# Alternating two token halves, and two PSUM banks, matmul by matmul, in a decoder trunk

## The chip, the cores and the metric

The kernel runs on one core of one Trainium2 chip. The metric is the device time of one execution in microseconds, as the median of several runs. A profile of one execution shows what each engine did: TensorE (PE for matmuls, PEld for the loading of stationary operands), VectorE (DVE), ScalarE (ACT), GpSimd (POOL) and the DMA queue of SyncE (SP).

## What is computed

A two-layer decoder trunk over 256 tokens with a model width of 2048, all in float32. Layer 0 projects into an RG-LRU group and an HGRN2 group, concatenates their outputs and projects back; layer 1 is attention with three dilated windows. Each is followed by a squared-ReLU MLP of width 8192. The large products are these:

```python
def trunk(x):                                   # x: 256 x 2048
    h = x + recurrent_mixers(rms(x), w_in, ..., w_out)    # w_in 2048 x 6144, w_out 2048 x 2048
    h = h + square(relu(rms(h) @ w1[0])) @ w2[0]          # w1 2048 x 8192, w2 8192 x 2048
    h = h + dilated_attention(rms(h), w_qkv, w_o)         # w_qkv 2048 x 6144, w_o 2048 x 2048
    h = h + square(relu(rms(h) @ w1[1])) @ w2[1]
    return rms(h)
```

## The kernel before

**Three products for one.** Weights and activations are float32, and each is held as a sum of two numbers of the faster matmul type: `hi`, the rounded value, and `lo`, the rest. A product is then three matmuls: high by high, high by low, low by high. The activations lie feature-major in `bufa` and `bufb` (128 partitions, 16 blocks of 128 features, the 256 tokens' high parts and then their low parts).

**Weights.** They come in units of 1 MB (128 x 2048) into `raw`, three buffers, on SyncE's queue. `Weights.split` (L97, L98) makes the two parts, in halves of 1024 columns: ScalarE casts `raw` to `hi`, VectorE subtracts to get `lo`. `hi` and `lo` have five half-unit buffers each, so a cast waits until TensorE has finished with the half that lay in its buffer, two and a half units back.

**Two kinds of product.** `project` keeps a weight block stationary and moves the 256 tokens; it fills one PSUM tile with 128 output features for all tokens, in some 5.5 us. `tokens` keeps activations stationary (128 features of 128 tokens) and moves 512 weight columns, and so fills two PSUM tiles, `ps[0]` for the first 128 tokens and `ps[1]` for the last 128, each one bank of 128 x 512 float32. Both take their tiles from the pool `pmm`, which has three, in turn; the five other banks belong to other pools. `tokens` is called for the HGRN and the attention values (`tokens_group`; evacuated by ScalarE at L314), for both output projections (`out_project`: w_out and w_o, four calls each), and for the MLP's second product (w2, four calls after each 16 calls of `project`, four times in a layer). A call goes through four units `g`, each with four blocks `i` of features: 4 x 4 x 2 halves x 3 products = 96 matmuls, 24 for each unit.

**Order.** All matmuls made by `mm` (L146) and the transposes made by `turn` (L149) are chained in program order on TensorE. The other engines' orders are laid out by the compiler by priority: evacuations are urgent, the weight stream comes next.

**After a call.** `add_res` (L553) adds `ps[0]` and then `ps[1]` to the residual `xres` on VectorE, one instruction for each half, which frees the two PSUM tiles. After `out_project`'s calls, and the last four of an MLP, the new columns are squared for the norm (L258) and transposed back to feature-major into `bufa` (`to_features`, L149, L203 and L204); that work is put off (`later`) and carried out by `flush` after the next call's first unit, or after 12 of the next `project`'s 16 blocks. The last four calls of the second MLP are multiplied by the final gain instead (L607), and each half's final norm (L719 to L725) and scaling (L729, L731) follow before the output DMAs (L733).

Of the kernel before, what the change touches and what calls it, by code (L numbers as in the profile page):

```python
# [19 lines left out]
P = 128  # L20
S = 256
# [19 lines left out]
def trunk_kernel(ctx, tc, x, xtok, cols, tab, masks, pos, fin, w_in, w_gate, w_out, w_qkv, w_o, w1, w2, out):  # L41
# [19 lines left out]
    bufa = act.tile([P, KB, 2 * S], F32R, name="bufa")  # L61
# [10 lines left out]
    for step in ORDER.split():  # L72
        src, first, n = where[step[0]]
# [9 lines left out]
    at = [0, 0]  # L83
# [51 lines left out]
    def unit(src, i):  # L135
        u = at[1]
        assert units[u][0] is src and units[u][1] == i, (u, i)
        at[1] += 1
        if u + 2 >= at[0]:
            fetch()  # L140
        return made.pop(u)
# [3 lines left out]
    def mm(*args, **kw):  # L145
        chain[:] = [after(T.matmul(*args, **kw), chain)]  # L146
# [6 lines left out]
    def flush():  # L153
        todo = later[:]
        later.clear()
        for f in todo:
            f()

    def after(ins, names):
        ins = getattr(ins, "ins", ins)  # L160
        for n in names:
            tc.add_manual_dep(ins, n, NOSYNC, reason="order on one engine")
        return ins.name
# [113 lines left out]
    def rstd(nrm):  # L277
        r = tmp.tile([P, 2], F32, name="nr2", bufs=2)
        rsqrt(r, nrm.mean(), 2)
        return r  # L280
# [7 lines left out]
            V.scalar_tensor_tensor(t, t, -0.5, v, op0=OP.mult, op1=OP.mult)  # L288
            V.scalar_tensor_tensor(r, t, 1.5, r, op0=OP.add, op1=OP.mult)

    def tokens(src, i0, mov, kgs=(0, 1, 2, 3), by_k=False):
        ps = [pmm.tile([P, 512], F32, name="p") for _ in range(2)]
        for g in kgs:
            w = unit(src, i0 + g)
            order = [(j, i) for i in range(4) for j in range(2)] if by_k else \
                [(j, i) for j in range(2) for i in range(4)]
            for j, i in order:
                k = 4 * g + i
                h, l = w.part(i * 512, 512)
                xh = mov[:, k, j * P:j * P + P]  # L300
                xl = mov[:, k, S + j * P:S + j * P + P]
                first, last = g == kgs[0] and i == 0, g == kgs[-1] and i == 3
                mm(ps[j], xh, h, start=first, stop=False)
                mm(ps[j], xh, l, start=False, stop=False)
                mm(ps[j], xl, h, start=False, stop=last)
            flush()
        return ps

    def tokens_group(src, i0, rt=None, by_k=False):
        ps = tokens(src, i0, bufa, by_k=by_k)  # L310
        v = vgs.tile([P, 2, 512], F32, name="vg", bufs=2)
        with urgent():
            for j in range(2):
                A.activation(v[:, j], ps[j], AF.Copy, scale=1.0 if rt is None else rt[:, j:j + 1])  # L314
        return v
# [16 lines left out]
    rt = rstd(nrm)  # L332
# [64 lines left out]
        return t.rearrange("p (n two c) -> p n two c", two=2, c=c)[:, :, int(second), :]  # L397

    def hgrn_v(i):
        v = tokens_group(w_in, 16 + i * 16, rt if i else None, by_k=not i)  # L400
        if not i:
            for j in range(2):
                A.activation(v[:, j], v[:, j], AF.Copy, scale=rt[:, j:j + 1])
        return v
# [133 lines left out]
    for step in ORDER.split():  # L538
        i = int(step[1])
        if step[0] == "v":  # L540
            vgroups[i] = hgrn_v(i)
        elif step[0] == "h":
            hgrn(i, vgroups[i // 4])
        else:
            {"x": lru_in, "y": lru_out, "g": lru_gates}[step[0]](i)
# [26 lines left out]
    def out_project(src, gname, kgs):  # L572
        nrm = Norm()
        for n in range(4):
            add_res(tokens(src, 4 * n, bufb, kgs), n, nrm)
            to_features(n, gname)
        return nrm
# [6 lines left out]
    def mlp(layer, nrm, nxt, gname):  # L584
        r2 = None
        for q in range(4):
            for m in range(16):
                z = folded(project(w1, layer * 64 + q * 16 + m, bufa), "z")
                with urgent():
                    V.scalar_tensor_tensor(z, z, 0.0, z, op0=OP.max, op1=OP.mult)  # L590
                    split_to(bufb[:, m], z)
                if r2 is None:
                    r2 = nrm.inv_mean()
                    if not gname:
                        lut(spare, epsc, AF.Sqrt)
                    spot[:] = [after(V.memset(spare, 0.0), [])]
            for n in range(4):
                ps = tokens(w2, layer * 64 + q * 16 + 4 * n, bufb)
                add_res(ps, n, nxt if q == 3 else None, r2)
                if q == 3:  # L600
                    if gname:
                        to_features(n, gname)
                    else:
                        at = slice(n * 512, n * 512 + 512)
                        with urgent():
                            for j in range(2):
                                V.tensor_tensor(xres[:, j, at], xres[:, j, at], fing[:, at], OP.mult)  # L607
# [36 lines left out]
    rt = rstd(nx1)  # L644
# [46 lines left out]
    for g in range(4):  # L691
        if g < 3:
            vg = tokens_group(w_qkv, g * 12, rt)
        for hd in range(4 * g, 4 * g + 4):
            u0 = g * 12 + (4 if g < 3 else 0) + (hd % 4) * 2
            st = scores(u0)
            if g < 3:
                mix(hd, st, vg)
            else:
                pend.append(st)  # L700
    vg = tokens_group(w_qkv, 44, rt)
    for hd, bank in zip(range(12, 16), (("po", 1), ("pd", 1), ("pl", 2), ("pl", 2))):
        mix(hd, pend[hd - 12], vg, *bank)
# [10 lines left out]
    for j in range(2):  # L714
        m = tmp.tile([P, 1], F32, name="fm", bufs=2)
        r = tmp.tile([P, 1], F32, name="fr", bufs=2)
        t = tmp.tile([P, 1], F32, name="ft", bufs=2)
        with urgent():
# [7 lines left out]
            for h in range(4):  # L726
                at = slice(h * 512, h * 512 + 512)
# [113 lines left out]
```

## Time and profile before

| | |
|---|---|
| median of 3 runs | 2237.13 us (2237.09 to 2237.16) |
| the profiled execution | 2237.57 us, span 2235.8 us, granted clock 0.999 |
| PE busy | 2218.4 us, 99% of the span, 12196 matmuls |
| PEld busy | 1935.1 us, 87%, 12196 loads |
| DVE busy | 1410.6 us, 63% |
| ACT busy | 1074.4 us, 48% |
| matmuls `p<-hi,bufb` and `p<-lo,bufb` of 128 x 512 (w2, w_out, w_o) | 2560 of 390 ns and 1280 of 389 ns |
| casts to `hi` (L97), splits to `lo` (L98) of 128 x 1024 | 770 of 1051 ns, 770 of 1223 ns |
| `add_res` (L553), with and without a scale | 64 of 748 ns, 16 of 688 ns |

A matmul's row is its whole passage, and the next one begins before it ends, so rows of 390 ns follow each other closer than that; starts are compared, not durations. In a tile's name the operand named first after the arrow is the moving one: `p<-hi,bufb` moves high weights over stationary activations. A number in brackets at the end of a row of the timeline is the idle time of the engine before it, with what ended it.

### The profile page before, as it was taken

The numbers are of one execution on the slowest core, as the hardware profiler recorded it, in microseconds if no ns is written. First come the engines' busy times: TensorE is split into PE (matmuls) and PEld (weight loads), VectorE is DVE, ScalarE is ACT, GpSimd is POOL, SyncE is SP. The second block draws the span as 40 slices with busy tenths as digits, with TensorE's granted clock in tenths as the row PEclk, the third lists the DMA queues.
The fourth block names the chain that finished last, engine by engine and source line by source line (L and its number), as shares of the span: only waits on it lengthen the run. The fifth ranks groups of instructions, "written<-read, shape, count | busy, mean of one in ns | idle before, by whom it ended". The sixth has DMA issues, their size and how long they took to land.

```text
span 2235.8 us, 30376 instructions
## 1 busy us (share of the span) xinstructions
PE 2218.4 (99%) x12196; PEld 1935.1 (87%) x12196; DVE 1410.6 (63%) x2220; ACT 1074.4 (48%) x1540; POOL 1.9 (0%) x7
## 2 busy tenths in 40 slices
PE   9999999999999999999999999999999999999998
PEld 8999998888888888888888888888888888888886
DVE  7777886665565565465567878556655645655654
ACT  6444585554444344354554445455434434444543
POOL 0000000000000000000000000000000000000000
PEclk9999999999999999999999999999999999999999
DMA  8444445455555555555554444555555555555553
GB/s 309 151 154 168 152 154 205 172 191 191 200 188 188 190 190 189 199 193 188 188 188 167 172 170 170 191 186 188 189 188 191 191 193 196 189 188 190 190 192 125
DMA packets 58717, 414.51 MB, mean 185 GB/s; under 512 B 6528, under 2 KB 7296, under 8 KB 9168
## 3 DMA queue, kind: packets, MB, share of 16 engines
q1 hardware_dynamic: 58320, 412.20, 51.9%
q8 instruction: 95, 1.56, 0.3%
q0 software_dynamic: 256, 0.38, 0.1%
q14 instruction: 46, 0.38, 0.1%
HBM read 410.70 MB, written 2.10 MB: 185 GB/s over the span
## 4 chain that ended last, share of the span: by engine, by line
PE 98%; ACT 1%; DVE 1%; DMA 0%; issue 0%; SPq 0%; ACTq 0%; DVEq 0%
PE p L146 94%; PE pl L440 1%; PE pl L149 0%; PE pl L665 0%; DMA raw<-in_w_in 0%; PE po L686 0%; PE pd L678 0%; ACT hi L97 0%; DVE bufa L204 0%; ACT L169 0%; DVE lo L98 0%; PE pd L424 0%; PE pl L664 0%; ACT gi L169 0%; PE po L687 0%
## 5 line engine op out<-in xcount | busy, mean ns | idle before, releaser
L98 DVE TENSOR_TENSOR lo<-raw,hi 128x1024 fp32r<-128x1024 f32 (+1 forms) x774 | 932.5, 1220 | 602.7 <-ACT hi L97 435.2
L97 ACT CAST hi<-raw 128x1024 fp32r<-128x1024 f32 (+1 forms) x774 | 811.3, 1049 | 876.7 <-PE p L146 798.7
L146 PE MATMUL p<-bufa,hi 128*128 128x512 f32 (+1 forms) x3840 | 858.2, 357 | 2.4 <-DVE bufa L204 2.4
L146 PE MATMUL p<-hi,bufb 128*128 128x512 f32 x2560 | 792.5, 390 | 0.0
L146 PEld LDWEIGHTS p<-bufa,hi 128*128 128x128 f32 x3840 | 671.9, 189 | 94.8 <-DVE bufa L204 3.5
L146 PEld LDWEIGHTS p<-hi,bufb 128*128 128x128 f32 x2560 | 480.7, 188 | 99.1
L146 PE MATMUL p<-bufa,lo 128*128 128x256 f32 x3200 | 520.0, 284 | 0.0
L146 PE MATMUL p<-lo,bufb 128*128 128x512 f32 x1280 | 498.1, 389 | 0.0
L146 PEld LDWEIGHTS p<-bufa,lo 128*128 128x128 f32 x3200 | 451.9, 191 | 12.3
L146 PEld LDWEIGHTS p<-lo,bufb 128*128 128x128 f32 x1280 | 240.4, 188 | 49.2
L201 DVE TENSOR_TENSOR bufb<-z,bufb 128x256 fp32r<-128x256 f32 x136 | 57.7, 424 | 126.5 <-ACT bufb L200 126.5
L146 PE MATMUL p<-hi,bufa 128*128 128x512 f32 x384 | 122.5, 395 | 0.5 <-ACT hi L97 0.5
L193 ACT COPY t<-p 128x256 f32<-128x256 f32 x128 | 47.6, 372 | 110.0 <-PE p L146 110.0
L146 PEld LDWEIGHTS p<-hi,bufa 128*128 128x128 f32 x384 | 72.2, 188 | 16.1 <-ACT hi L97 1.5
L146 PE MATMUL p<-lo,bufa 128*128 128x512 f32 x192 | 76.4, 398 | 1.6 <-DVE lo L98 1.6
L200 ACT CAST bufb<-z 128x256 fp32r<-128x256 f32 x136 | 54.5, 401 | 17.2 <-DVE z L590 14.4
L553 DVE SCALAR_TENSOR_TENSOR xall<-p,nm,xall 128x512 f32<-128x512 f32 x64 | 47.9, 748 | 19.8 <-PE p L146 19.8
L590 DVE SCALAR_TENSOR_TENSOR z<-z 128x256 f32<-128x256 f32 x128 | 54.5, 426 | 4.4
L195 DVE TENSOR_TENSOR z<-p,t 128x256 f32<-128x256 f32 x128 | 53.5, 418 | 0.0
L258 ACT ACTIVATE z<-xall 128x512 bf16<-128x512 f32 x32 | 20.2, 631 | 53.3 <-DVE xall L553 52.6
L146 PEld LDWEIGHTS p<-lo,bufa 128*128 128x128 f32 x192 | 36.1, 188 | 10.3 <-DVE lo L98 3.6
L440 PE MATMUL pl<-qk 128*128 128x64 f32 x224 | 30.9, 260 | 0.0
(199 smaller groups left out, 730.1 us busy)
## 6 DMA issues: line engine op xcount, KB each, us to landing
raw<-in_w SPq DMA_DIRECT2D x256, 1024.0 KB, 4.8
raw<-in_w_qkv SPq DMA_DIRECT2D x48, 1024.0 KB, 4.8
raw<-in_w_in SPq DMA_DIRECT2D x46, 1024.0 KB, 4.8
raw<-in_w_out SPq DMA_DIRECT2D x16, 1024.0 KB, 4.8
raw<-in_w_o SPq DMA_DIRECT2D x16, 1024.0 KB, 4.8
xall<-in_xtok SPq DMA_DIRECT2D x1, 2048.0 KB, 9.3
raw<-in_w_gate SPq DMA_DIRECT2D x2, 1024.0 KB, 4.8
out<-xall SPq DMA_DIRECT2D x4, 512.0 KB, 3.3
```

Source lines behind the costliest of these rows:

```text
L97: A.copy(h, w)
L98: V.tensor_tensor(l, w, h.bitcast(F32), OP.subtract)
L146: chain[:] = [after(T.matmul(*args, **kw), chain)]
L193: A.copy(t, p[:, S:])
L195: V.tensor_tensor(z, p[:, :S], t, OP.add)
L200: A.copy(dst[:, :S], src)
L201: V.tensor_tensor(dst[:, S:], src, dst[:, :S].bitcast(F32), OP.subtract)
L258: A.activation(q, xres[:, j, n * 512:n * 512 + 512], AF.Square, accum_out=self.ss[:, j, n:n + 1])
L440: T.matmul(pl[:, j], kq[:, js], halves(qp[:, js], c, True), start=True, stop=True)
L553: V.scalar_tensor_tensor(xres[:, j, at], ps[j], 1.0 if scale is None else scale[:, j:j + 1], xres[:, j, at], op0=OP.mult, op1=OP.add)
L590: V.scalar_tensor_tensor(z, z, 0.0, z, op0=OP.max, op1=OP.mult)
```

## The change

In `tokens` the loop over the two halves becomes the innermost. Before, each unit went through all four blocks for the first half (12 matmuls into `ps[0]`) and then for the second (12 into `ps[1]`); the first HGRN value group alone (`by_k`) changed halves after each block's three products. After, for each block and each of the three products, one matmul goes into `ps[0]` and the next into `ps[1]`. The number of matmuls, their operands and their shapes are the same. Within a unit, the first half of the weights (blocks 0 and 1) is used by the first 12 matmuls instead of by matmuls 1 to 6 and 13 to 18. The argument `by_k` goes.

```diff
-    def tokens(src, i0, mov, kgs=(0, 1, 2, 3), by_k=False):
+    def tokens(src, i0, mov, kgs=(0, 1, 2, 3)):
         ps = [pmm.tile([P, 512], F32, name="p") for _ in range(2)]
         for g in kgs:
             w = unit(src, i0 + g)
-            order = [(j, i) for i in range(4) for j in range(2)] if by_k else \
-                [(j, i) for j in range(2) for i in range(4)]
-            for j, i in order:
+            first, last = g == kgs[0], g == kgs[-1]
+            for i in range(4):
                 k = 4 * g + i
                 h, l = w.part(i * 512, 512)
-                xh = mov[:, k, j * P:j * P + P]
-                xl = mov[:, k, S + j * P:S + j * P + P]
-                first, last = g == kgs[0] and i == 0, g == kgs[-1] and i == 3
-                mm(ps[j], xh, h, start=first, stop=False)
-                mm(ps[j], xh, l, start=False, stop=False)
-                mm(ps[j], xl, h, start=False, stop=last)
+                for n, (at, m) in enumerate(((0, h), (0, l), (S, h))):
+                    for j in range(2):
+                        mm(ps[j], mov[:, k, at + j * P:at + j * P + P], m, start=first and not i and not n,
+                           stop=last and i == 3 and n == 2)
             flush()
         return ps
```

`tokens_group` and `hgrn_v` lose the argument `by_k` that they passed on.

More of the change, by code (lines that the diff above doesn't have):

```diff
@@ L294, in tokens, with tokens_group @@
             w = unit(src, i0 + g)
-            order = [(j, i) for i in range(4) for j in range(2)] if by_k else \
-                [(j, i) for j in range(2) for i in range(4)]
-            for j, i in order:
+            first, last = g == kgs[0], g == kgs[-1]
+            for i in range(4):
                 k = 4 * g + i
                 h, l = w.part(i * 512, 512)
-                xh = mov[:, k, j * P:j * P + P]
-                xl = mov[:, k, S + j * P:S + j * P + P]
-                first, last = g == kgs[0] and i == 0, g == kgs[-1] and i == 3
-                mm(ps[j], xh, h, start=first, stop=False)
-                mm(ps[j], xh, l, start=False, stop=False)
-                mm(ps[j], xl, h, start=False, stop=last)
+                for n, (at, m) in enumerate(((0, h), (0, l), (S, h))):
+                    for j in range(2):
+                        mm(ps[j], mov[:, k, at + j * P:at + j * P + P], m, start=first and not i and not n,
+                           stop=last and i == 3 and n == 2)
             flush()
         return ps
-    def tokens_group(src, i0, rt=None, by_k=False):
-        ps = tokens(src, i0, bufa, by_k=by_k)
+    def tokens_group(src, i0, rt=None):
+        ps = tokens(src, i0, bufa)
         v = vgs.tile([P, 2, 512], F32, name="vg", bufs=2)
@@ L399, in hgrn_v @@
     def hgrn_v(i):
-        v = tokens_group(w_in, 16 + i * 16, rt if i else None, by_k=not i)
+        v = tokens_group(w_in, 16 + i * 16, rt if i else None)
         if not i:
```

## The prediction

> **What bounds the kernel now.** I read the busy shares and the chain of the page first, then the timeline around one boundary between two token groups, then the places where TensorE really waits.
>
> ```profile
> PE 2218.4 (99%) x12196; PEld 1935.1 (87%) x12196; DVE 1410.6 (63%) x2220; ACT 1074.4 (48%) x1540; POOL 1.9 (0%) x7
> PEclk9999999999999999999999999999999999999999
> PE 98%; ACT 1%; DVE 1%; DMA 0%; issue 0%; SPq 0%; ACTq 0%; DVEq 0%
> ```
>
> TensorE is the path, at full clock (0.999 granted), so the end moves only if the spacing of its matmuls changes or if a new idle gap opens. PE and PEld have the same count: every matmul loads its own weights, also where two in a row have the same stationary block, so the change breaks up no shared load. The next fence is TensorE's timeline across the boundary of two groups of `tokens` (the last matmul of one starts at 538.67, the first of the next 0.23 later, inside the same row of two).
>
> ```profile
> 537.99 0.61 PE L146 MATMUL p<-hi,bufb 128*128 128x512 f32 x2
> 538.44 0.39 PE L146 MATMUL p<-lo,bufb 128*128 128x512 f32 x1
> 538.67 0.61 PE L146 MATMUL p<-hi,bufb 128*128 128x512 f32 x2
> 539.12 0.39 PE L146 MATMUL p<-lo,bufb 128*128 128x512 f32 x1
> 539.35 0.61 PE L146 MATMUL p<-hi,bufb 128*128 128x512 f32 x2
> 539.80 0.39 PE L146 MATMUL p<-lo,bufb 128*128 128x512 f32 x1
> ```
>
> Triples follow each other every 0.68 us, 226.7 ns a matmul, and the one that holds a change of bank is no different. VectorE over the same place:
>
> ```profile
> 536.38 0.75 DVE L553 SCALAR_TENSOR_TENSOR xall<-p,nm,xall 128x512 f32<-128x512 f32 x1 [0.41 <-PE p L146]
> 538.82 1.22 DVE L98 TENSOR_TENSOR lo<-raw,hi 128x1024 fp32r<-128x1024 f32 x1 [1.69 <-ACT hi L97]
> 539.96 0.74 DVE L553 SCALAR_TENSOR_TENSOR xall<-p,nm,xall 128x512 f32<-128x512 f32 x1
> 540.62 1.22 DVE L98 TENSOR_TENSOR lo<-raw,hi 128x1024 fp32r<-128x1024 f32 x1
> ```
>
> The first half's tile is evacuated (L553) 39 ns after its last matmul, which is the 12th before the end of the group; the second half's waits 0.9 us behind a weight split. Neither delays TensorE: `ps[1]` of the next group is not touched before that group's 13th matmul.
>
> **Steady rate: no change (0 us).** `tokens` is called 46 times with 96 matmuls, 4416 of the 12196. In the six undisturbed w2 stretches I took the start-to-start time at each of the 96 positions: where the bank changes (after every 12th) it is 226.6 ns, elsewhere 226.5 to 226.8 (the first five of a group up to 229). A wide matmul has a fixed part of 13 ns: 512 columns take 226.7, 256 take 120.0, so 256 columns are 106.7 and 226.7 - 2 x 106.7 = 13.3. If it came from writing the same bank twice running, it would be gone at each of those changes; it isn't.
>
> **New wait: the third buffer.** `pmm` has three tiles, handed out in turn (the compiled kernel before takes banks 0, 2, 1 throughout). A group holds A and B; the next gets C, then A. Before, A's last matmul and its next first one are 24 matmuls (5.4 us) apart. After, they are three apart: A last, B last, C first, A first. Between the two lies the evacuation of A. Call C's first start 0, by rows:
> - A's last matmul starts two steps earlier, at -0.453, and its row is 0.389 long: end -0.064.
> - L553 starts 0.039 later and takes 0.751 (w2) or 0.692 (w_out, w_o; no scale): end 0.726 or 0.667.
> - TensorE restarts 0.053 after it, as here, where a matmul waits for VectorE (L204 ends at 431.255, in the run of four from 430.77):
>
> ```profile
> 431.31 0.49 PE L146 MATMUL p<-bufa,hi 128*128 128x512 f32 x1 [0.65 <-DVE bufa L204]
> 430.77 1.95 DVE L204 SCALAR_TENSOR_TENSOR bufa<-pl,c__82,bufa 128x256 fp32r<-128x256 f32 x4
> 431.31 0.19 PEld L146 LDWEIGHTS p<-bufa,hi 128*128 128x128 f32 x1 [0.89 <-DVE bufa L204]
> ```
>
> The matmul and its weight load start together: the wait holds the load back too, so the load is exposed. The matmul is 0.49 long instead of 0.39, and after the second such wait (432.335) the next two start 0.337 and 0.236 later instead of 0.227: 0.12 us more. So A's first matmul starts at 0.779 instead of 0.227: 0.55 + 0.12 = 0.67 us a boundary in w2, 0.61 in w_out and w_o.
>
> Boundaries: 3 in each of 8 w2 passes, 24 x 0.67 = 16.1; 3 each in w_out and w_o, 6 x 0.61 = 3.7; the last value group of w_qkv is followed directly by w_o, there ScalarE evacuates (L314, 0.687): 0.6. Where a feature-major `project` stands on either side there is no cost: it uses one tile for about 5.5 us, and the tile that is needed has long been read.
>
> **Who else stands in VectorE's queue.** Each unit's 24 matmuls free the first half of its weights at the 18th matmul before, at the 12th after; ScalarE's cast (L97) and VectorE's split (L98) hang on that and move 6 x 0.227 = 1.36 us earlier. The split above ends at 540.04; moved, at 538.68. A's last matmul ends at 538.81, so L553 finds VectorE free, by 0.13 us. That margin is thin; without it the wait grows up to the 0.91 by which the second L553 is late now (its rival is below).
>
> **Ends of the kernel.** At the end, the first half's L553, final gain, norm and scaling run under the last 12 matmuls today. After, both halves come together: 0.75 + 0.69 (L607) + 2 x 0.48 (L731) + 7 x 0.16 = 3.5 us of VectorE work is moved behind the last matmul, of which part fills VectorE's idle time between 2225.3 and 2230.9, where it waits for ScalarE. Between 0 and 3.5 I take 1.5, nearer to the lower half because the second half's chain is mostly waits. At the start, the group already alternated by threes; one more matmul gets ahead of the wait for `lo` at 21.66: -0.2 (bounds -0.7, three such waits, and 0). The residual transposes (L149) come after the next group's first 24 matmuls, 5.4 us, and both L553 are done after 1.5: nothing.
>
> **Sum.** 16.1 + 3.7 + 0.6 + 1.5 - 0.2 = 21.7 us. The profiled execution took 2237.57 (span 2235.8): 2259.3; it lies 0.44 above the median, so the prediction is 2237.1 + 21.7 = 2258.8. Without the exposed load and the tail (31 x 0.12 + 1.5 less) it is 2253.6.
>
> A rule speaks against the change: the Trainium skill, "Perfetto Trace Analysis", section "Matmuls", asks that independent groups rotate through banks so that the evacuation of one overlaps the next one's matmuls. The trace before shows just that; with two groups open and three banks there is one bank left to rotate into.
>
> **Rivals.**
> - *Banks help, faster.* If writing alternate banks takes the fixed 13.3 ns off every matmul, 4416 x 13.3 = 58.7 less, 21.7 more: 2200. It wins once a step falls by 21.7 / 4416 = 4.9 ns, below 221.8. For it: the fixed part has no explanation in the rows. Against: 226.6 at every existing change of bank. Chance 0.08. The Trainium skill, "TensorE: Matmul & The Clock Gate", section "Back-to-back issue gap", gives N/2.4 + 2.5, 215.7 ns for 512 columns; the trace shows 11 more, and an estimate by that page would be 4416 x 11 = 48.6 us less if the change recovered it.
> - *The split stays in front of L553.* VectorE's order is fixed when the kernel is compiled; if the moved split starts 0.13 us or more too late, L553 begins up to 0.91 late at each of 31 boundaries: up to 28 more, 2268 to 2287. For it: this is what the second L553 shows before. Against: the earlier release. Chance 0.12.
> - *No wait.* Bank A is read in time after all, or the change alters no order that matters: 2236 to 2240. Against: 0.75 of evacuation can't fit in the 0.29 us between A's last end and its next start. Chance 0.04.
>
> **Numbers.** Forecast (the wait of 0.55 to 0.8 at about 31 boundaries, 2252 to 2268): 0.76. With the second rival slower is 0.88; 0.2% (4.5 us) is about what a measurement can tell from no change. The range 2252 to 2282 takes in the forecast and most of the second rival.
>
> **What would show it.** The waits view should have about 24 "PE p L146 <- DVE xall L553" of 0.5 to 0.6 us, 13 in sum, and six or seven smaller; TensorE's busy time nearly unchanged, triples still every 0.68 us. Rows of 512 columns closer than 222 ns would prove me wrong on the banks, waits of 1.5 us with L98 in front of L553 on the queue, no waits for L553 at all on the buffers.

## Result and profile after

The changed kernel takes 2262.23 us (2262.11 to 2262.34) against 2237.14 (2237.09 to 2237.16): 1.0112 times as long, 95% interval 1.0095 to 1.013, 25.1 us more. The profiled execution has a span of 2260.5 against 2235.8, 24.7 more (the execution profiled before lay 0.4 above its median); the lines of the changed kernel stand three earlier (`add_res` is L550). From the page after, the busy times, the clock and the chain:

```profile
PE 2228.0 (99%) x12196; PEld 1931.5 (85%) x12196; DVE 1409.8 (62%) x2220; ACT 1072.0 (47%) x1540; POOL 1.9 (0%) x7
PEclk9999999999999999999999999999999999999999
PE 95%; DVE 2%; ACT 2%; issue 0%; DMA 0%; SPq 0%; ACTq 0%; DVEq 0%
```

The same work at the same clock. TensorE's share of the chain fell from 98% to 95%; VectorE's and ScalarE's rose from 1% to 2% each, and `add_res` (L550), which the chain's list of lines did not have before, now stands in it with 1%: something waits for it. TensorE's timeline over the boundary that the prediction showed, now 2.66 us later:

```profile
540.65 0.62 PE L146 MATMUL p<-lo,bufb 128*128 128x512 f32 x2
541.11 0.84 PE L146 MATMUL p<-hi,bufb 128*128 128x512 f32 x3
542.34 0.50 PE L146 MATMUL p<-hi,bufb 128*128 128x512 f32 x1 [0.39 <-DVE xall L550]
542.68 0.64 PE L146 MATMUL p<-lo,bufb 128*128 128x512 f32 x2
```

The row of three holds the last two matmuls of one group and the first of the next. Then the second of the next group, which wants the tile A, starts at 542.34, 0.779 us after the first; before, the distance was 0.227. It is 0.50 long instead of 0.39, and the next starts 0.341 later instead of 0.227. VectorE and the weight loads there:

```profile
540.13 1.23 DVE L98 TENSOR_TENSOR lo<-raw,hi 128x1024 fp32r<-128x1024 f32 x1 [1.50 <-ACT hi L97]
541.53 1.41 DVE L550 SCALAR_TENSOR_TENSOR xall<-p,nm,xall 128x512 f32<-128x512 f32 x2 [0.18 <-PE p L146]
```

```profile
542.34 0.19 PEld L146 LDWEIGHTS p<-hi,bufb 128*128 128x128 f32 x1 [0.81 <-DVE xall L550]
```

VectorE has finished its split and stands idle for 0.18 us until A's last matmul ends; then both halves are added one behind the other. The load for A's first matmul waits with the matmul. The waits view collects it:

```profile
PEld p L146 <- DVE xall L550: 24.8, 31, 0.8
PE p L146 <- DVE xall L550: 11.8, 31, 0.4
PEld p L146 <- DVE z L377: 1.7, 1, 1.7
```

A column of 11.8 us for TensorE undersells it: idle time counts from the modelled end of the matmul before, which lies 0.39 after its start, while the pace is a start every 0.227. The starts of the same matmul in both traces say what each place costs:

| where | later by, us |
|---|---|
| start and first HGRN value group | -0.9 |
| first w_out group, a wait for the tile of the last y block but one | 1.65 |
| 24 boundaries of w2, 0.69 to 0.73 each | 16.9 |
| 3 + 3 boundaries of w_out and w_o, 0.63 to 0.67 each | 3.9 |
| w2's last group to the first value group of w_qkv | 0.7 |
| last value group of w_qkv to the first w_o group | 0.6 |
| after the last matmul | 1.8 |

They add to the 24.7. At the first w_out group TensorE waits for VectorE's evacuation of a y block (L377); at the first w_o group it waits for ScalarE's evacuation of the value group (L311):

```profile
336.57 0.50 PE L146 MATMUL p<-hi,bufb 128*128 128x512 f32 x1 [1.38 <-DVE z L377]
336.10 0.42 DVE L377 TENSOR_TENSOR z<-p,nr 128x256 f32<-128x256 f32 x1
1438.21 0.70 PE L683 MATMUL po<-pT,vg 128*128 128x256 f32 x2 [0.33 <-ACT vg L311]
```

The matmul that waits in the last row is not w_o's second one but a product of the attention heads that reads the evacuated values `vg`. Before, it stood behind w_o's first eleven matmuls; now it stands behind the first alone. All other stages have the same length in both to within 0.06 us, and between the 31st and the last matmul of an undisturbed group the mean distance of two starts is 226.67 ns in both traces.

### The profile page after: what moved, and what is told of

Read it like the earlier page. It is cut to its first block, busy times and chain, and to the rows that moved or that the text cites. A ratio compares the mean times of both kernels' runs of the same rounds, so it can differ in the third digit from the quotient of the medians.

```text
span 2260.5 us, 30371 instructions
## 1 busy us (share of the span) xinstructions
PE 2228.0 (99%) x12196; PEld 1931.5 (85%) x12196; DVE 1409.8 (62%) x2220; ACT 1072.0 (47%) x1540; POOL 1.9 (0%) x7
## 4 chain that ended last, share of the span: by engine, by line
PE 95%; DVE 2%; ACT 2%; issue 0%; DMA 0%; SPq 0%; ACTq 0%; DVEq 0%
PE p L146 92%; DVE xall L550 1%; PE pl L437 1%; ACT hi L97 0%; PE pl L149 0%; PE pl L662 0%; ACT L169 0%; PE po L683 0%; DVE lo L98 0%; ACT gi L169 0%; PE pd L675 0%; DMA xall<-in_x 0%; ACT bufa L203 0%; DVE bufa L204 0%; PE pd L421 0%
## 5 line engine op out<-in xcount | busy, mean ns | idle before, releaser
L146 PE MATMUL p<-hi,bufb 128*128 128x512 f32 x2560 | 697.7, 391 | 12.8 <-DVE xall L550 11.4
L146 PE MATMUL p<-lo,bufb 128*128 128x512 f32 x1280 | 394.9, 390 | 0.0
L146 PE MATMUL p<-hi,bufa 128*128 128x512 f32 x384 | 109.1, 396 | 1.2 <-ACT hi L97 0.8
L146 PE MATMUL p<-lo,bufa 128*128 128x512 f32 x192 | 60.1, 394 | 1.1 <-DVE lo L98 1.1
L550 DVE SCALAR_TENSOR_TENSOR xall<-p,nm,xall 128x512 f32<-128x512 f32 x64 | 45.1, 746 | 16.5 <-PE p L146 16.1
L437 PEld LDWEIGHTS pl<-qk 128*128 128x128 f32 x224 | 30.1, 191 | 0.3
```

The costliest lines, as they stand in the source:

```text
L437: T.matmul(pl[:, j], kq[:, js], halves(qp[:, js], c, True), start=True, stop=True)
L550: V.scalar_tensor_tensor(xres[:, j, at], ps[j], 1.0 if scale is None else scale[:, j:j + 1], xres[:, j, at], op0=OP.mult, op1=OP.add)
```

## Experiments

The theory: the loss is the evacuation of A, between two matmuls that the new order brings within three of each other, plus the waits and the tail that come from both halves ending together. The rival: alternating banks or stationary blocks at every matmul is slow by itself.

**Four tiles, and the control for it.** The edit in the changed kernel, and in the kernel before:

```diff
-    pmm = pool("pmm", 3, space=PSUM)
+    pmm = pool("pmm", 4, space=PSUM)
...
-        p = psc.tile([P, 512], F32, name="pt", bufs=1)
+        p = psc.tile([P, 512], F32, name="pd", bufs=1)
...
-        pt = psc.tile([P, 2, P], F32, name="pt", bufs=1)
+        pt = psc.tile([P, 2, P], F32, name="pd", bufs=1)
```

> The changed kernel with four tiles in the pool pmm instead of three (the bank comes from the tile pt, whose uses move to pd). Theory (A's evacuation sits between two matmuls that are only three apart): with four tiles the next group takes two others, no matmul waits for add_res, the 24.7 us between the two traces shrink to the tail (+1.8) and the start (-0.9): about 2238 us. Rival (writing two banks alternately, or changing the stationary block every time, is slow by itself): all matmuls still alternate, so it stays at about 2262.

> The kernel before with the same four tiles in pmm and pt merged into pd. Control for the other run: the kernel before waits nowhere for a tile of pmm, so both theories expect 2237 us, within 0.5, unless sharing pd costs something in the HGRN heads; what it costs there has to be taken off the other run too.

Measured: 2291.29 us (2290.71 to 2292.64) and 2290.79 (2290.21 to 2291.23). Both totals missed: merging `pt` into `pd` costs the kernel before 53.7 us. But the two differ by 0.5 us where the kernels they come from differ by 25, and between their traces no boundary from the second w_out group on is longer; only the tail is, by 1.82. So the loss goes when neighbouring groups share no tile, though the control's own cost makes this a weak proof, and the last run below repeats it without that. Where the 53.7 arise can be seen on the page of the control:

```profile
PEclk9999977999999999999999999999999999999999
```

and by its waits in the HGRN heads:

```profile
PEld pd L478 <- ACT ho L475: 9.5, 2, 5.6
```

From 300 to 320 us TensorE is busy 10.3 of 20 us, with 36 matmuls at a granted clock of 0.50, where the kernel before is busy all 20, with 169 matmuls at 1.00. Sharing the tile leaves the heads' small dependent products without other matmuls to cover them; the clock falls to a half over two stretches, 34 and 27 us long. How much of the 53.7 is the waits and how much the clock, no run separates.

**Alternate in three units of four.** The matmuls of a unit are listed and, in one unit of the group, sorted by half:

```diff
+            steps = [(i, n, j) for i in range(4) for n in range(3) for j in range(2)]
+            if last:                                  # in the other run: if first
+                steps.sort(key=lambda s: s[2])
-            for i in range(4):
+            for i, n, j in steps:
...
```

> The changed kernel, but in the last of a group's four units the first half's 12 matmuls come before the second half's, as in the kernel before; 72 of 96 matmuls alternate. Theory: A's last matmul is now 14 matmuls (3.2 us) before its next first one, against 0.75 of evacuation: no wait between groups, and no longer tail; the wait of 1.65 us for the last y block's tile at the first w_out group stays, and the start gains 0.9: 2237 to 2238.5 us. Rival (alternating is slow by itself): three quarters of the loss stay, about 2256.

> The changed kernel, but in the first of a group's four units the first half's 12 matmuls come first; 72 of 96 alternate. Theory: A is first needed at the 13th matmul, 14 after its last: no wait between groups and none for the last y block's tile; the tail of 1.8 us stays since both halves end together, the start gains between 0 and 0.9: 2238 to 2239.5 us. Rival (alternating is slow by itself): about 2256.

Measured: 2238.64 us (2238.34 to 2238.89), 1.0007 of before (0.9998 to 1.0016), and 2238.68 (2238.3 to 2239.37), 1.0007 (0.9998 to 1.0017); the first lies 0.1 above the range that was expected, the second within. Neither has a wait for `add_res` on TensorE, although three quarters of the matmuls still alternate: the rival, with 2256 for both, is out. Against the trace before, the first is later only at the first w_out group, by 1.64, and the second only after the last matmul, by 1.84. Either end of the group alone is enough to give the evacuation its room; which end is left decides which of the two smaller losses stays.

**By threes, and one block by halves.** The same list, sorted otherwise:

```diff
-                steps.sort(key=lambda s: s[2])
+                steps.sort(key=lambda s: (s[0], s[2], s[1]))                      # by threes, in every unit
+                steps.sort(key=lambda s: (s[0], s[2] if not s[0] else 0, s[1], s[2]))   # first block, first unit
```

> The changed kernel, but halves (and banks) change after each block's three products instead of after every matmul. Theory: A's last matmul starts 4 steps (0.907 us) before the next group and its next first one 3 steps (0.680) after its start; A is free again at -0.907 + 0.389 + 0.039 + 0.751 + 0.053 = 0.325, so no wait between groups. The wait for the last y block's tile shrinks by two steps to about 1.2, the tail is 1.5 to 1.8 longer than before: about 2240 us. Rival (every change of half or bank costs): a third as many changes as in the changed kernel, so a third of the loss, about 2245, and no waits to be seen.

> The changed kernel, but the first block of a group's first unit does its three products for the first half, then for the second; the other 90 matmuls alternate. Theory in numbers: A is free for loading at 0.779 us (w2) or 0.719 (w_out, w_o) after the group's start and is now wanted at 0.680: a wait of 0.10 or 0.04 stays, and with it the restart of 0.12 to 0.16: about 0.24 us at 25 boundaries and 0.18 at 7, 1.2 for the last y block, 1.8 of tail, -0.9 at the start: 2246 us. If the weight load were not held back by the wait, the restart would be missing: 2242.

Measured: 2240.78 us (2240.64 to 2241.0), 1.0017 (1.0008 to 1.0026), and 2247.48 (2247.23 to 2247.72), 1.0046 (1.0031 to 1.0061). By threes no boundary between groups costs more than 0.06 us and no wait for `add_res` shows; together the boundaries still come to 1.2, as the starts behind each are up to 12 ns further apart than 227 for some ten matmuls, which was not expected and stays unexplained. The rest is 1.19 at the first w_out group and 1.39 of tail, less 0.5 at the start. With one block by halves each boundary costs 0.23 to 0.27 us in w2 and 0.17 to 0.21 in w_out and w_o, against 0.24 and 0.18 expected; the total lies 1.5 above the 2246 that was expected. The remaining wait itself is 0.10 in w2 (A's first matmul starts 0.326 us after its predecessor instead of 0.227), so more than half of the cost is the restart (the next starts follow after 0.341, 0.240 and 0.235). The waits view names the loads (`add_res` is L552 in this run):

```profile
PEld p L146 <- DVE xall L552: 10.8, 31, 0.4
```

All 31 are still there, and on average the load unit stood idle 0.35 us ahead of them, for matmuls that were 0.04 to 0.10 late: the load was not made beforehand. This is the run that separates the restart from the wait: without it about 2242 was expected.

**A longer evacuation.** In three of four w2 passes:

```diff
         with urgent():
+            if not nrm:
+                twice = tmp.tile([P, S], F32, name="z").bitcast(BF16)
+                V.tensor_copy(twice, ps[0])
             for j in range(2):
                 V.scalar_tensor_tensor(xres[:, j, at], ps[j], ...
```

> The changed kernel with one more VectorE instruction, a copy of ps[0] to an idle bf16 tile, ahead of add_res in the first three w2 passes of each layer (not the fourth). Theory: at the 18 boundaries inside those passes A becomes free later by the whole length of the copy, 0.6 to 0.7 us, all of it on the path: 11 to 13 us more than the changed kernel, 2273 to 2275 us. Rival (TensorE waits for something else, and add_res only ends at the same time): no or little change, 2262 to 2264.

Measured: 2273.14 us (2272.84 to 2273.23), 10.9 more than the changed kernel. VectorE and TensorE at the boundary shown above, in this run (L551 is the copy, L553 `add_res`):

```profile
541.81 0.69 DVE L551 CAST z<-p 128x512 bf16<-128x512 f32 x1 [0.18 <-PE p L146]
542.41 1.40 DVE L553 SCALAR_TENSOR_TENSOR xall<-p,nm,xall 128x512 f32<-128x512 f32 x2
```

```profile
543.21 0.50 PE L146 MATMUL p<-hi,bufb 128*128 128x512 f32 x1 [0.99 <-DVE xall L553]
```

The idle time went from 0.39 to 0.99 with the 0.60 by which `add_res` starts later (L553 starts 0.60 behind the copy, which took its place). The 18 boundaries with the copy cost 1.28 to 1.33 us each, the other six of w2 still 0.69 to 0.73. What TensorE waits for is this evacuation, one for one.

**The first group alone.** The kernel before, with the new order in the first HGRN value group:

```diff
-            order = [(j, i) for i in range(4) for j in range(2)] if by_k else \
-                [(j, i) for j in range(2) for i in range(4)]
+            steps = [(i, n, j) for i in range(4) for n in range(3) for j in range(2)]
+            if not by_k:
+                steps.sort(key=lambda s: s[2])
...
```

> The kernel before, with the new inner order in the first HGRN value group alone (which alternated by threes). Theory: the start's gain comes from this order, one more matmul ahead of each wait for a split: 0.6 to 0.9 us faster than before, 2236.2 to 2236.5, with nothing else moved. Rival (the start differs from execution to execution, with the transfers): 2237.1.

Measured: 2236.79 us (2236.62 to 2237.08) against 2237.08 (2236.84 to 2237.45), 0.9999 (0.999 to 1.0007). Between both expectations and not to be told from no change. The traces agree: the first group ended 0.46 us earlier than in the trace before here, but 0.49 earlier in the run by threes, where its order is the old one. The start differs between executions by as much as the order could bring.

**A fourth tile outside the HGRN heads.** The changed kernel, every matmul alternating, with every second call of `tokens` in w_out, w_o and w2 taking its second tile from `pt`:

```diff
-        ps = [pmm.tile([P, 512], F32, name="p") for _ in range(2)]
+        ps = [pmm.tile([P, 512], F32, name="p") for _ in range(1 if spare else 2)]
+        if spare:
+            ps.append(psc.tile([P, 512], F32, name="pt", bufs=1))
...
```

> The changed kernel with a fourth tile only in w_out, w_o and w2: every second call of tokens takes its second half's tile from pt, which is idle there, and the HGRN heads keep pt as they had it. All matmuls alternate as in the changed kernel. Theory: neighbouring groups share no tile, so the waits of 24 + 6 boundaries and the one into the first attention group are gone; what stays is 1.65 for the last y block's tile, 0.63 into the first w_o group, 1.84 of tail, and -0.3 to -0.9 at the start: 2240.5 to 2241. Rival (alternating is slow by itself): 2262.

Measured: 2240.91 us (2240.73 to 2241.21), 1.0018 (1.0008 to 1.0027). The boundary, in this run (the row of three again holds the last two matmuls of one group and the first of the next; `add_res` is L552):

```profile
539.45 0.84 PE L146 MATMUL p<-hi,bufb 128*128 128x512 f32 x3
540.12 0.39 PE L146 MATMUL pt<-hi,bufb 128*128 128x512 f32 x1
540.35 0.39 PE L146 MATMUL p<-lo,bufb 128*128 128x512 f32 x1
```

```profile
539.87 1.41 DVE L552 SCALAR_TENSOR_TENSOR xall<-p,nm,xall 128x512 f32<-128x512 f32 x2 [0.18 <-PE p L146]
```

The next group's second matmul takes `pt` and starts 0.227 us after its first, while VectorE evacuates both halves. Against the trace before, only three places are later: 1.64 at the first w_out group, 0.63 at the first w_o group (ScalarE evacuates there, and the tile is still shared), 1.82 of tail. So 21.3 of the 25.1 us were the tiles that neighbouring groups share, in a kernel whose matmuls are in the changed order throughout.

## Why the prediction was right, and where it was off

- **Steady rate, 0 us:** right. 226.67 ns in both traces, and 2240.91 with every matmul alternating. Changing the bank at every matmul takes nothing off the fixed 13 ns, so the rival of 2200 us is out, and with it the 48.6 us of the estimate beside it; what the 13 ns are stays open.
- **The wait at a w2 boundary, 0.67:** the mechanism and its arithmetic held to the last step, A's first matmul at 0.778 to 0.780 at every boundary of w2, where 0.779 was worked out. The term that was too small is the restart: 0.12 was taken, 0.16 measured (0.71 - 0.55), because the starts after the wait stay slightly apart for some ten matmuls (341, 240, 235, 233, 236 ns...) and the prediction counted two. Over 24 boundaries that is 0.8 us, and 0.2 over the six of w_out and w_o (0.65 against 0.61).
- **The count of boundaries, 31:** two were missed. The last w2 group of layer 0 is followed directly by the first value group of w_qkv (0.7). And the sentence that a `project` on either side costs nothing failed at the first w_out group: it argued that the tile needed has long been read, from the length of a `project`, and did not look at VectorE's queue. There VectorE, busy without a pause with the y blocks' elementwise work and weight splits, reaches the evacuation of the last y block but one (L377; the expectations call it the last) at 336.10, while w_out wants its tile at 335.03; the order before asked for it 2.5 us later in the group. That one place costs 1.65 us, more than two boundaries. At the first w_o group 0.6 was right: the evacuation that is waited for is the one that the prediction took, though it had w_o's second matmul wait for it and not a product of the heads.
- **VectorE's queue:** right. The split moved ahead as worked out; L550 started 37 to 39 ns after A's last matmul at every boundary, with VectorE idle for 0.13 to 0.18 us before it. (The prediction's 538.81 for the end of A's last matmul is 538.83 by its own rows, and the margin there 0.15 instead of 0.13.) The rival with the split in front (2268 to 2287) did not happen.
- **Tail, 1.5:** 1.8 measured. **Start, -0.2:** -0.9 in the one trace, but two runs with the old order at the start also began 0.3 and 0.5 earlier than the trace before, so that much can be the difference of executions; what the order adds stays open, below what was measured.
- **The sum:** 21.7 was said, 24.7 is the difference of the traces. The parts of the difference: 0.8 + 0.2 for restarts, 0.7 + 1.65 for missed places, 0.3 for the tail, less 0.7 at the start: 3.0.
- **How it would show:** 31 waits are there (24 in w2, six in w_out and w_o, one into w_qkv), but as 0.39 us each on TensorE (11.8 in all, not 13 and more from 24), because the prediction took the delay of a start for idle time, which begins only at the modelled end of the matmul before.

## What to carry to other kernels

Before interleaving two accumulation groups, count buffers, not banks: with two groups open, the next two need both of their tiles at once, and the last matmul of one group and the first of another on the same tile come as close as the interleaving is fine. Compare the time between their two starts with the last matmul, the evacuation and the two delays between them (here 0.39 + 0.04 + 0.75 + 0.05 us); interleaving by threes, or ending (or starting) each group half by half, cost 1.5 to 3.7 us in all here, against 25.1. And walk through every place where one group follows something else: the dearest single wait stood where VectorE was busy with another stage.

## What the runs showed of the hardware

A held-back matmul costs more than its wait: a wait of 0.10 us at a boundary cost 0.23 to 0.27. In the changed kernel, at 542.34, the weight load and its matmul start together and the next start is 0.34 later instead of 0.227: the load is held with the matmul. Giving up one PSUM tile in a stage of small dependent products cost 53.7 us, and the granted clock stood at 0.50 for 61 us of that trace. It first fell at 298.7 us, in the fourth of four idle gaps of 0.8 to 1.5 us with 0.6 to 0.7 us of short products between them; the gaps of 0.4 us at the boundaries of the changed kernel left it at 1. No run varies the gaps, so where the limit lies stays open.
